# One pool of weight staging buffers for a two-layer hybrid backbone on one core, with feed-forward groups of 512, 512 and 256 tokens

## The chip, the cores and the metric

The kernel runs on 1 core of a Trainium2 chip: TensorE (PE in the rows) multiplies matrices, VectorE (DVE), ScalarE (ACT) and GpSimd (POOL) work elementwise, SyncE (SP) issues the DMA transfers, and 16 DMA engines move data between memory and the core. Each engine works off its own instructions in order and waits on semaphores for the others. The metric is the device time of one execution in microseconds.

## The reference, cut to what matters

```python
for l in range(DEPTH):                       # 2 layers, D_MODEL 1024, D_FF 4096
    mod_l = silu(c) @ w_mod[l] + b_mod[l]    # six vectors: shift, scale, gate, twice; mod_c from c_ctx
    h_l = rms_norm(x, norm1_g[l]) * (1 + sc1_l) + sh1_l        # 1024 latent tokens
    h_c = rms_norm(xc, norm1_g[l]) * (1 + sc1_c) + sh1_c       # 256 context tokens
    pl, pc = split_cols(h_l @ w_in[l]), split_cols(h_c @ w_in[l])
    ...                                      # four mixers: convolution, gated scan, attention, retention
    x = x + g1_l * (concatenate([y_conv, y_gla, y_att, y_ret]) @ w_out[l])
    h2_l = rms_norm(x, norm2_g[l]) * (1 + sc2_l) + sh2_l
    x = x + g2_l * (square(relu(h2_l @ w_up[l])) @ w_down[l])
    if l < DEPTH - 1:
        ...                                  # the same for the context xc
return rms_norm(x, final_norm_g)             # latent tokens only
```

The weights of the second layer's modulation, `w_mod[1]`, are multiplied while the feed-forward of the first layer runs.

## The kernel before

**Tokens and products.** The stream is kept transposed, features on the partitions, in three groups of tokens (`TOK`): t = 0 is the context with 256 tokens, t = 1 and t = 2 hold 512 latent tokens each. Every large fp32 product is done as three matmuls of rounded parts (`mm3`, L189): high times high, high times low, low times high. The trace shows them in the order `ahi,whi`, `alo,whi`, `ahi,wlo` (moving, weights); all matmuls have line L187. In a layer come the projections with the attention, the scans, the output projection and the feed-forward.

**How weights arrive.** `load_slab` (L250) takes a staging tile `wst`, lets SyncE load a slab of weights into it (L258) and calls `split`: ScalarE casts it to the high part `whi` (L180), VectorE subtracts to the low part `wlo` (L181). When the low part is done, the staging tile is free for the next load. In the wide phase (`open_w`: output projection and feed-forward, slabs of 1024 columns, 512 KB) and in the narrow phase (`open_narrow`: projections and attention, slabs of 512 or 544 columns) there are 3 staging tiles, and each phase has its own, in the pool of the weights. The modulation slabs (`stage_w`, L274, named `wm`) go through the same tiles; TensorE reads them straight from the tile in fp32, and the tile is free when those matmuls are done.

**The feed-forward.** The 4096 hidden features are cut into 16 chunks of 256. A unit is one chunk with one token group, in the order chunk, then t = 0, 1, 2 (layer 1 has only t = 1, 2). For each unit the loop takes two steps of the modulation generator `mg` (`emit_mods`, L310; it hands out 8 slabs, one step each, and then one step that evaluates and transposes, six times over, 54 steps in all, which with two steps a unit last through the first nine chunks of layer 0; in layer 1 `mg` is empty). Then it emits `up` of the next unit and `down` of this one:

```python
1199        for i, u_ in enumerate(units):
1200            step(mg, 2)
1201            if i + 1 < len(units):
1202                up(*units[i + 1])
1207            down(*u_)
```

`up` loads the chunk's two w_up slabs when t is the first group, and `down` its two w_down slabs. An up or a down is 48 matmuls of 512 columns (256 for t = 0).

**The layer boundary.** Behind the last chunk, `next_norm` forms the next layer's first norm for each group: ScalarE squares, VectorE adds (L369), TensorE sums over the partitions (`c<-acc,ones`), ScalarE makes the factor (L174), VectorE and ScalarE apply it (L382, L385, L386). Then the attention's slabs come (two granules of four slabs with 512 columns), and `att_in` multiplies them with tiles of 128 tokens: 0 and 1 are the context, 2 to 9 the latents. The order of emission, a little rearranged by a scheduler at build time, is the order on each engine.

Of the kernel before, what the change touches and what calls it, by code (L numbers as in the profile page):

```python
# [8 lines left out]
F32 = mybir.dt.float32  # L9
# [3 lines left out]
ALU = mybir.AluOpType  # L13
# [7 lines left out]
NTILE = NT // 128  # L21
CT = NCTX // 128
FF = 4096
P_IN = 2576
EPS = 1e-6
FC = 256
SLAB = 1024
NSLAB = 544
TOK = [(0, 256), (256, 512), (768, 512)]
C_CONV, C_GLA, C_GLAZ, C_GATE_R, C_ATT, C_RET, C_GATE_G = 0, 512, 1280, 1024, 1296, 1808, 2320  # L30
# [70 lines left out]
def build(tc, a, out, dbg=None):  # L101
    cst = a["cst"]
    nc = tc.nc
    pools = Pools(tc)
    PS = bass.MemoryType.PSUM
    dbg = dbg or {}

    cpool = pools.get("cpool")
    nrm = pools.get("nrm", bufs=2)
    xyp = {}  # L110

    def open_xy():
        xyp[0] = xyp[1] = pools.get("xy01")
        xyp[2] = pools.get("xy2")

    dram = pools.get("dram", space=bass.MemoryType.DRAM)
    P = {}
# [58 lines left out]
            after_(i_, cur["load"])  # L176
            cur["users"].append(i_)

    def split(hi, lo, src):
        nc.scalar.copy(hi, src)  # L180
        nc.vector.tensor_tensor(lo, src, hi.bitcast(F32), op=ALU.subtract)  # L181

    def tr(ps, src, n=128):
        nc.tensor.transpose(ps, src, ident[:n, :n])  # L184
# [52 lines left out]
    W = {}  # L237

    def open_w():
        wp = pools.get("wp", bufs=5)  # L240
        W.update(pools=[wp], group=1, n=0, width=SLAB, st=wp, stages=3)

    def open_narrow(**kw):
        wps = [pools.get(nm, bufs=4, **kw) for nm in ("wpa", "wpb")]
        W.update(pools=wps, group=4, n=0, width=NSLAB, st=wps[0], stages=3)

    def close_narrow():
        pools.close("wpb", "wpa")

    def load_slab(src, k, n):  # L250
        wd_ = W["width"]
        st = W["st"].tile([128, wd_], F32, tag="wst", name="wst", bufs=W["stages"])
        if not isinstance(src, list):
            src = [(src, n)]
        o = 0
        v = st[:, :k * n].rearrange("p (k n) -> p k n", k=k)
        for s, w in src:
            nc.sync.dma_start(out=v[:, :, o:o + w], in_=s)  # L258
            o += w
        p = W["pools"][W["n"] // W["group"] % len(W["pools"])]  # L260
        W["n"] += 1
        hi = p.tile([128, wd_], F32R, tag="whi", name="whi")
        lo = p.tile([128, wd_], F32R, tag="wlo", name="wlo")
        split(hi[:, :k * n], lo[:, :k * n], st[:, :k * n])
        return (hi[:, :k * n].rearrange("p (k n) -> p k n", k=k), lo[:, :k * n].rearrange("p (k n) -> p k n", k=k))

    def granule(l, pieces, width):
        w_in = a["w_in"][l].rearrange("(k p) n -> p k n", p=128)
        return [load_slab([(w_in[:, 2 * q:2 * q + 2, c0:c0 + w], w) for c0, w in pieces], 2, width) for q in range(4)]

    def att_cols(g):
        return [(C_ATT + 128 * g, 128), (C_ATT + 256 + 64 * g, 64), (C_ATT + 384 + 64 * g, 64)]

    def stage_w():  # L274
        v = W["st"].tile([128, W["width"]], F32, tag="wst", name="wm", bufs=W["stages"])
        return v[:, :512 if W["width"] < 1024 else 1024].rearrange("p (k q n) -> p k q n", k=1, q=4)

    vecs = [cpool.tile([128, NV], F32, name=f"vec{l}") for l in range(2)]
    wdw = [cpool.tile([128, 62], F32, name=f"wdw{l}") for l in range(2)]
# [70 lines left out]
    def xy_tile(t, nm):  # L350
        return xyp[t].tile([128, KD, TOK[t][1]], F32, tag=f"xy{t}", name=f"{nm}{t}")
# [43 lines left out]
    xin = pools.get("xin", bufs=2)  # L395
# [49 lines left out]
    for t in (2, 0, 1):  # L445
        for k in range(0, KD, 2):
            nc.sync.dma_start(out=xdram[:, k:k + 2, TOK[t][0]:TOK[t][0] + TOK[t][1]], in_=xt[t][:, k:k + 2, :])
    pools.close("xin", "init", "xy2", "xy01", "psd")

    pace = []  # L450

# [16 lines left out]
    for l in range(2):  # L468
        last = l == 1
# [110 lines left out]
        def att_in(A, i, sls, aa, tb):  # L580
# [55 lines left out]
            nc.sync.dma_start(out=attraw[i][:, h0 * 64:320], in_=ov[:, 1, h0:5, :].rearrange("p h d -> p (h d)"))  # L636
            att_prep(A, i, ov[:, 0].rearrange("p h d -> p (h d)"))

        def att_stage(sls, *others):
            aa = pools.get("aa", bufs=2)  # L640
            tb = {"cos": aa.tile([128, 8, 32], F32, name="cosa", bufs=1), "sin": aa.tile([128, 8, 32], F32, name="sina", bufs=1),
                  "gain": aa.tile([128, 2, 3, 64], F32, name="gain", bufs=1)}
            nc.sync.dma_start(out=tb["cos"].rearrange("p a b -> p (a b)"), in_=cslice("cosatt"))
            nc.sync.dma_start(out=tb["sin"].rearrange("p a b -> p (a b)"), in_=cslice("sinatt"))
            for g in range(2):
                for h_ in range(3):
                    src = a["att_q_norm_g" if h_ < 2 else "att_k_norm_g"][l:l + 1, :]
                    nc.sync.dma_start(out=tb["gain"][:, g, h_, :], in_=src.to_broadcast([128, 64]))
            A = att_tiles()
            for _ in stagger((att_in(A, i, sls, aa, tb) for i in range(NTILE)), 2):  # L650
                for g_ in others:
                    step(g_)
            pools.close("aa")
            return A

        def att_second(A):
            for i in range(NTILE):
                h0 = 0 if need_q(i) else 2
                rw = at_.tile([128, 256], F32, tag="arw", name="arw", bufs=2)
                nc.sync.dma_start(out=rw[:, h0 * 64:256], in_=attraw[i][:, h0 * 64:256])  # L660
                nc.sync.dma_start(out=A["ve"][:, i, :], in_=attraw[i][:, 256:320])
                att_prep(A, i, rw)
                yield
# [7 lines left out]
        def attend(A, g):  # L671
            qa, ka, kb, ve = A["qa"], A["ka"], A["kb"], A["ve"]
            nfill = 0
            for t in order:
# [45 lines left out]
                nc.vector.reciprocal(ls[:, 0:nt, :], ls[:, 0:nt, :])  # L720
                rb = bank("pt")
                for j in range(nt):
                    dg = at_.tile([128, 2, 128], F32, tag="adg", name="adg")
                    nc.vector.tensor_tensor(dg, ident[:, None, :].to_broadcast([128, 2, 128]),
                                            ls[:, j, :].unsqueeze(2).to_broadcast([128, 2, 128]), op=ALU.mult)
                    for h_ in range(2):
                        mm(rb[64 * h_:64 * h_ + 64, j * 128:(j + 1) * 128], ones[:, 0:64], dg[:, h_, :], True, True)
# [6 lines left out]
        n_att = sum(len(tiles_of(t)) * (3 + (CT if t == 0 else NTILE) // 2) + 1 for t in tts)  # L734
        n_tok = sum(TOK[t][1] for t in tts)

        A = att_stage(first if l == 0 else [granule(l, att_cols(g), 256) for g in range(2)], mg)
        at_ = pools.get("at", bufs=2)


# [57 lines left out]
        def gla_in(i, qk):  # L798
# [43 lines left out]
            b = bank("s")  # L842
            for d_ in range(2):
                tr(b[:, d_ * 128:(d_ + 1) * 128], ke[:, d_, :])
            kt = ag.tile([128, 2, 128], F32, tag="ket", name="ket")
            nc.vector.tensor_copy(kt, b[:, 0:256].rearrange("p (a b) -> p a b", a=2))
            yield
            outer(b, 256, kt, st, i, ag, glakv)
# [89 lines left out]
        pools.close("ar", "actp", "at", "ap", "pss", "psa", "psd")  # L938
        close_narrow()
        open_xy()  # L940
        y = [None if last and t == 0 else xy_tile(t, "y") for t in range(3)]
        for t in tts:
            o, n = TOK[t]
            nc.sync.dma_start(out=y[t][:, 4:6, :], in_=yatt[:, :, o:o + n])
# [182 lines left out]
        w_up = a["w_up"][l].rearrange("(k p) n -> p k n", p=128)  # L1127
        w_dn = a["w_down"][l].rearrange("(f p) n -> p f n", p=128)
        NF = FC // 128
        units = [(c, t) for c in range(FF // FC) for t in tts]  # L1130
        wu, wd, hid = {}, {}, {}

        def up(c, t):
            n = TOK[t][1]
            if t == tts[0]:
                wu[c] = [load_slab(w_up[:, :, (c * NF + f) * 128:(c * NF + f + 1) * 128], 8, 128) for f in range(NF)]
            hi, lo = h2[t]
            hh = hp.tile([128, NF, 512], F32R, tag="hh", name="hh")
            hl = hp.tile([128, NF, 512], F32R, tag="hl", name="hl")
            for f in range(NF):  # L1140
                b = bank()
                uh, ul = wu[c][f]
                mm3(b[:, :n], [(uh[:, k, :], ul[:, k, :], hi[:, k, :], lo[:, k, :]) for k in range(KD)])
                rl = ntmp()
                nc.scalar.activation(rl[:, :n], b[:, :n], AF.Relu)  # L1145
                nc.scalar.activation(hh[:, f, :n], rl[:, :n], AF.Square)  # L1146
                nc.vector.tensor_tensor(rl[:, :n], rl[:, :n], rl[:, :n], op=ALU.mult)  # L1147
                nc.vector.tensor_tensor(hl[:, f, :n], rl[:, :n], hh[:, f, :n].bitcast(F32), op=ALU.subtract)
            hid[c, t] = (hh, hl)

        def down(c, t):
            n = TOK[t][1]
            seg = 1 if t == 0 else 0
            if t == tts[0]:
                wd[c] = [load_slab(w_dn[:, c * NF + f:c * NF + f + 1, :], 1, 1024) for f in range(NF)]
            hh, hl = hid.pop((c, t))
            for d in range(8):
                ds = slice(d * 128, (d + 1) * 128)
                b = bank()
                mm3(b[:, :n], [(wd[c][f][0][:, 0, ds], wd[c][f][1][:, 0, ds], hh[:, f, :n], hl[:, f, :n]) for f in range(NF)])  # L1160
                nc.vector.scalar_tensor_tensor(xt[t][:, d, :], b[:, :n], mod(l, 5, d, seg), xt[t][:, d, :], op0=ALU.mult, op1=ALU.add)  # L1161
                if c == FF // FC - 1:
                    if d == 0:
                        acc[t] = nacc()
                    square(acc[t], xt[t][:, d, :], n, d == 0)
# [47 lines left out]
        if "x" in dbg and dbg.get("l", 0) == l:  # L1213
            for t in tts:
                o, n = TOK[t]
                nc.sync.dma_start(out=dbg["x"][:, :, o:o + n], in_=xt[t])
        pools.close("hp", "wp", "xy2", "xy01", "psd")
    pools.close("actp", "dram", "nrm", "cpool")


def _layout(inputs):
# [26 lines left out]
```

## Time and profile before

| | |
|---|---|
| median of 3 runs (lowest, highest) | 3265.65 us (3259.18, 3268.56) |
| the profiled execution, its span | 3255.2 us, 3253.4 us |
| TensorE, VectorE, ScalarE, GpSimd busy | 94%, 51%, 28%, 2% of the span |
| mean granted clock of TensorE | 0.963 of full speed |
| feed-forward of layer 0 | about 883 to 1806.5 us |
| layer boundary | 1806.5 to about 1850 us |
| feed-forward of layer 1 | about 2527 to 3230 us |

Times in the rows are microseconds from the start of the span. A granted clock of 1.00 is 2.4 GHz, 0.50 is 1.2 GHz. A share of busy time is a mean over stages with different limits, so that the stages are to be read one by one. Idle time in brackets behind a row is that of the engine just before the instruction, with what ended it.

### The profile page before, as it was taken

What the parts mean: (1) busy time and instruction counts of PE and PEld (TensorE: products, weight loads), DVE (VectorE), ACT (ScalarE), POOL (GpSimd) and SP (SyncE); (2) the same over time, 40 slices, a digit from 0 to 9 for tenths busy, and PEclk for the clock granted to TensorE, in tenths of its full rate; (3) what the DMA queues carried; (4) which work ended last, traced back from release to release, by engine and by line L of the source; (5) the groups of instructions that cost most, each with busy time, mean ns of one, the idle gap of its engine ahead of it and who ended that gap; (6) DMA issues with size and microseconds to landing.
All of it is one profiled execution on the core that took longest, in us unless ns stands there. A gap on an engine that the chain in (4) does not pass through costs nothing. (4 is left out here: it accounts for less than half of the span.)

```text
span 3253.4 us, 43496 instructions
## 1 busy us (share of the span) xinstructions
PE 3055.0 (94%) x18101; PEld 2446.2 (75%) x18101; DVE 1672.7 (51%) x2660; ACT 912.7 (28%) x1650; POOL 66.0 (2%) x114
## 2 busy tenths in 40 slices
PE   7899899868999999999999799999769999999998
PEld 4777677646888888888888777677537788888887
DVE  4559633343654444444545659633444644444545
ACT  4322343242321121121112433343332221112222
POOL 0200000000000000000000010000000000000000
PEclk8899999878999999999999799999889999999999
DMA  8422412362122222221110310212531211111111
GB/s 267 121 69 90 119 49 71 97 196 94 51 79 85 91 85 78 79 65 39 40 39 1 99 55 30 78 47 72 174 117 58 64 51 41 39 52 52 52 39 52
DMA packets 267230, 250.32 MB, mean 77 GB/s; under 512 B 28258, under 2 KB 227512, under 8 KB 267032
## 3 DMA queue, kind: packets, MB, share of 16 engines
q1 hardware_dynamic: 266616, 246.61, 24.1%
q8 instruction: 142, 2.33, 0.3%
q0 software_dynamic: 416, 0.92, 0.1%
q14 instruction: 56, 0.46, 0.0%
HBM read 200.42 MB, written 47.05 MB: 76 GB/s over the span
## 5 line engine op out<-in xcount | busy, mean ns | idle before, releaser
L187 PE MATMUL bank<-ahi,whi 128*128 128x512 f32 (+1 forms) x2096 | 794.7, 379 | 13.7 <-ACT ahi L180 11.2
L187 PE MATMUL bank<-ahi,wlo 128*128 128x512 f32 (+1 forms) x2096 | 786.3, 376 | 2.5 <-DVE wlo L181 2.5
L187 PE MATMUL bank<-alo,whi 128*128 128x512 f32 (+1 forms) x2096 | 787.3, 376 | 0.0
L1161 DVE SCALAR_TENSOR_TENSOR x<-bank,mods,x 128x512 f32<-128x512 f32 (+1 forms) x640 | 439.2, 695 | 253.1 <-PE bank L187 251.6
L187 PEld LDWEIGHTS bank<-ahi,whi 128*128 128x128 f32 x2096 | 396.6, 189 | 110.2 <-ACT ahi L180 14.0
L187 PE MATMUL bank<-hl,whi 128*128 128x512 f32 (+1 forms) x1280 | 472.1, 369 | 0.0
L187 PE MATMUL bank<-hh,whi 128*128 128x512 f32 (+1 forms) x1280 | 471.6, 368 | 0.0
L187 PE MATMUL bank<-hh,wlo 128*128 128x512 f32 (+1 forms) x1280 | 471.0, 368 | 0.0
L187 PEld LDWEIGHTS bank<-ahi,wlo 128*128 128x128 f32 x2096 | 396.1, 189 | 82.0 <-issue 6.0
L187 PEld LDWEIGHTS bank<-alo,whi 128*128 128x128 f32 x2096 | 396.6, 189 | 75.5 <-issue 5.4
L180 ACT CAST whi<-wst 128x1024 fp32r<-128x1024 f32 (+2 forms) x226 | 199.6, 893 | 675.5 <-PE bank L187 492.5
L181 DVE TENSOR_TENSOR wlo<-wst,whi 128x1024 fp32r<-128x1024 f32 (+2 forms) x226 | 232.3, 1039 | 285.1 <-ACT whi L180 283.1
L1145 ACT ACTIVATE tmp<-bank 128x512 f32<-128x512 f32 (+1 forms) x160 | 88.3, 552 | 659.8 <-PE bank L187 658.4
L187 PEld LDWEIGHTS bank<-hh,whi 128*128 128x128 f32 x1280 | 241.3, 188 | 40.9
L187 PEld LDWEIGHTS bank<-hl,whi 128*128 128x128 f32 x1280 | 241.3, 189 | 40.6 <-issue 0.2
L187 PEld LDWEIGHTS bank<-hh,wlo 128*128 128x128 f32 x1280 | 241.3, 189 | 40.4 <-issue 0.2
L1147 DVE TENSOR_TENSOR tmp<-tmp 128x512 f32<-128x512 f32 (+1 forms) x160 | 102.0, 639 | 312.0 <-ACT hh L1146 310.2
L187 PE MATMUL bank<-whi,ahi 128*128 128x256 f32 (+2 forms) x640 | 197.4, 309 | 8.1 <-ACT whi L180 3.5
L187 PE MATMUL bank<-wlo,ahi 128*128 128x256 f32 (+2 forms) x640 | 191.2, 299 | 0.2 <-DVE wlo L181 0.2
L187 PE MATMUL bank<-whi,alo 128*128 128x256 f32 (+2 forms) x640 | 191.0, 298 | 0.0
L690 DVE TENSOR_REDUCE amx<-S 128x1 f32<-128x1280 f32 (+1 forms) x72 | 98.8, 1372 | 138.3 <-PE S L187 132.7
L520 DVE SCALAR_TENSOR_TENSOR yacc<-u,wdw,yacc 128x1295 f32<-128x1295 f32 (+1 forms) x120 | 168.4, 1421 | 0.8
(214 smaller groups left out, 3094.5 us busy)
## 6 DMA issues: line engine op xcount, KB each, us to landing
wm<-in_w_mod_dram SPq DMA_DIRECT2D x64, 512.0 KB, 3.8
wst<-in_w_up_dram SPq DMA_DIRECT2D x64, 512.0 KB, 3.8
wst<-in_w_down_dram SPq DMA_DIRECT2D x64, 512.0 KB, 4.1
wm<-in_w_mod_dram SPq DMA_DIRECT2D x64, 256.0 KB, 3.0
wst<-in_w_in_dram SPq DMA_DIRECT2D x48, 256.0 KB, 2.9
wst<-in_w_out_dram SPq DMA_DIRECT2D x16, 512.0 KB, 5.3
x<-xdram SPq DMA_DIRECT2D x4, 2048.0 KB
glaf<-gf SPq DMA_DIRECT2D x18, 384.0 KB, 2.5
```

What stands on the lines that cost most here:

```text
L180: nc.scalar.copy(hi, src)
L181: nc.vector.tensor_tensor(lo, src, hi.bitcast(F32), op=ALU.subtract)
L187: nc.tensor.matmul(ps, lhsT=lhsT, rhs=rhs, start=start, stop=stop)
L520: nc.vector.scalar_tensor_tensor(yv, uv, wv, yv, op0=ALU.mult, op1=ALU.add)
L690: nc.vector.reduce_max(mx[:, 0:1], S[:, 0:nk * 128], axis=AX.X)
L1145: nc.scalar.activation(rl[:, :n], b[:, :n], AF.Relu)
L1147: nc.vector.tensor_tensor(rl[:, :n], rl[:, :n], rl[:, :n], op=ALU.mult)
L1161: nc.vector.scalar_tensor_tensor(xt[t][:, d, :], b[:, :n], mod(l, 5, d, seg), xt[t][:, d, :], op0=ALU.mult, op1=ALU.add)
```

## The change

1. **One staging pool** `wst` for the whole program, with 2 tiles of 1088 columns. `stage_cols` hands out parts of a tile: slabs of 512 or 544 columns share one, two to a tile; a slab of 1024 columns (all of the feed-forward, its modulation slabs too) takes a whole one. So there are 2 stages instead of 3 in the wide phase and 4 half ones instead of 3 in the narrow phase.
2. **One pool** `xy` for the stream's tiles instead of two.
3. **The groups of layer 0's feed-forward** come as t = 1, 2, 0 (512, 512, 256 tokens) instead of 0, 1, 2. In layer 1 the attention's token tiles come as 2 to 9, then 0 and 1.
4. **The low parts** of layer 1's eight attention slabs are formed by GpSimd instead of VectorE.
5. **A pad** of 480 bytes a partition, and one buffer instead of two for three helpers (`arw` in the second half of the attention, `adg`, `ket`).

```diff
+STAGE = 1088
+    pools.get("pad", side="right").tile([128, 120], F32, name="pad")
     nrm = pools.get("nrm", bufs=2)
+    wstp = pools.get("wst", bufs=2)
     def open_xy():
-        xyp[0] = xyp[1] = pools.get("xy01")
-        xyp[2] = pools.get("xy2")
+        xyp[0] = xyp[1] = xyp[2] = pools.get("xy")
...
-    def split(hi, lo, src):
+    def split(hi, lo, src, lo_eng=None):
         nc.scalar.copy(hi, src)
-        nc.vector.tensor_tensor(lo, src, hi.bitcast(F32), op=ALU.subtract)
+        (lo_eng or nc.vector).tensor_tensor(lo, src, hi.bitcast(F32), op=ALU.subtract)
...
-        W.update(pools=[wp], group=1, n=0, width=SLAB, st=wp, stages=3)
+        W.update(pools=[wp], group=1, n=0, width=SLAB)
...
+    def stage_cols(n):
+        free = W.get("free")
+        if free is None or free[1] + n > STAGE:
+            free = [wstp.tile([128, STAGE], F32, tag="wst", name="wst"), 0]
+        v = free[0][:, free[1]:free[1] + n]
+        free[1] += n
+        W["free"] = free if free[1] < STAGE else None
+        return v
...
     def stage_w():
-        v = W["st"].tile([128, W["width"]], F32, tag="wst", name="wm", bufs=W["stages"])
-        return v[:, :512 if W["width"] < 1024 else 1024].rearrange("p (k q n) -> p k q n", k=1, q=4)
+        n = 512 if W["width"] < 1024 else 1024
+        return stage_cols(n).rearrange("p (k q n) -> p k q n", k=1, q=4)
...
+        tile_order = list(range(NTILE)) if l == 0 else list(range(CT, NTILE)) + list(range(CT))
...
-        A = att_stage(first if l == 0 else [granule(l, att_cols(g), 256) for g in range(2)], mg)
+        A = att_stage(first if l == 0 else [granule(l, att_cols(g), 256, nc.gpsimd) for g in range(2)], mg)
...
+        mt = [1, 2] if last else [1, 2, 0]
...
-        units = [(c, t) for c in range(FF // FC) for t in tts]
+        units = [(c, t) for c in range(FF // FC) for t in mt]
...
-            if t == tts[0]:
+            if t == mt[0]:
```

SyncE's issues at the first chunk boundary of layer 0's feed-forward, before. The number behind a name is the tile's own; `wm` are modulation slabs, three tiles turn over:

```order
L258 DMA wst_7901<-in_w_down_dram 128x1024
L323 DMA wm_7971<-in_w_mod_dram 128x4x256
L323 DMA wm_7977<-in_w_mod_dram 128x4x256
L323 DMA wm_8109<-in_w_mod_dram 128x4x256
L323 DMA wm_8115<-in_w_mod_dram 128x4x256
L258 DMA wst_8121<-in_w_up_dram 128x8x128
L258 DMA wst_8127<-in_w_up_dram 128x8x128
```

The same place after; now two tiles turn over, and all slabs bear the name `wst`:

```order
L269 DMA wst_7849<-in_w_down_dram 128x1024
L334 DMA wst_7919<-in_w_mod_dram 128x4x256
L334 DMA wst_7925<-in_w_mod_dram 128x4x256
L334 DMA wst_8057<-in_w_mod_dram 128x4x256
L334 DMA wst_8063<-in_w_mod_dram 128x4x256
L269 DMA wst_8069<-in_w_up_dram 128x8x128
L269 DMA wst_8075<-in_w_up_dram 128x8x128
```

The sequence is the same; what is other is the number of tiles, so that `wst_8069` and `wst_8075` stand two issues behind `wst_8057` and `wst_8063`, whose tiles they take.

TensorE at that boundary, before: the end of the down of group 1, the two modulation slabs, and the first matmuls with the new w_up slab, on the context's 256 tokens:

```order
L187 MATMUL bank_8101<-hl_7834,whi_7903 128x512
L187 MATMUL bank_8101<-hh_7833,wlo_7904 128x512
L187 MATMUL mo_7820<-wm_8109,scT_84 32x256 x4
L187 MATMUL mo_7820<-wm_8115,scT_84 32x256 x4
L187 MATMUL bank_8135<-ahi0_7400,whi_8123 128x256
L187 MATMUL bank_8135<-alo0_7401,whi_8123 128x256
L187 MATMUL bank_8135<-ahi0_7400,wlo_8124 128x256
```

And after, where the first group is t = 1 with 512 tokens:

```order
L189 MATMUL bank_8049<-hl_7782,whi_7851 128x512
L189 MATMUL bank_8049<-hh_7781,wlo_7852 128x512
L189 MATMUL mo_7768<-wst_8057,scT_91 32x256 x4
L189 MATMUL mo_7768<-wst_8063,scT_91 32x256 x4
L189 MATMUL bank_8083<-ahi1_7502,whi_8071 128x512
L189 MATMUL bank_8083<-alo1_7503,whi_8071 128x512
L189 MATMUL bank_8083<-ahi1_7502,wlo_8072 128x512
```

Directly behind the matmuls that read `wst_8057` and `wst_8063` stand those that need the slabs loaded into the same tiles.

TensorE at the layer boundary, before: the last down, the sum for the norm of group 2, and the first attention matmuls, on the context:

```order
L187 MATMUL bank<-hl,whi 128x512
L187 MATMUL bank<-hh,wlo 128x512
L187 MATMUL c_14666<-acc,ones 128x512
L187 MATMUL bank<-whi,ahi_14351 128x128 x2
L187 MATMUL bank<-wlo,ahi_14351 128x128
```

And after, where the first attention tile holds latent tokens:

```order
L189 MATMUL bank<-hl,whi 128x256
L189 MATMUL c_14489<-acc,ones 128x512
L189 MATMUL bank<-hh,wlo 128x256
L189 MATMUL c_14615<-acc,ones 128x256
L189 MATMUL bank<-whi,ahi_14299 128x256 x2
```

ScalarE there, after (`ahi_14487` is the normed group 2, `ahi_14613` group 0):

```order
L396 ACTIVATE ahi_14487<-tmp,mods_96 128x512 x8
L379 ACTIVATE tmp<-x_6821 128x256 x7
L176 ACTIVATE acc<-c_14615,eps 128x256
L176 ACTIVATE acc<-acc 128x256
L396 ACTIVATE ahi_14613<-tmp,mods_96 128x256 x8
L182 CAST whi<-wst 128x512 x8
```

Two sums now stand ahead of the attention on TensorE, the last that of the small group, and the eight casts stand behind both norms; before, the first cast stood between the two activations of the last norm.

## Rows read from the trace of the kernel before

**Rows 1.** The page: span, and TensorE's busy time, share and instructions.
```profile
span 3253.4 us, 43496 instructions
PE 3055.0 (94%) x18101; PEld 2446.2 (75%) x18101; DVE 1672.7 (51%) x2660; ACT 912.7 (28%) x1650; POOL 66.0 (2%) x114
```

**Rows 2.** Chain of waits, its last long link: start, length, engine, tile, line, instructions.
```profile
2528.25 692.27 PE bank L187 x3005
```

**Rows 3.** Stretches: busy time (instructions) by engine, granted clock, DMA share, GB/s.
```profile
core 0: us, PE busy (x) PEld busy (x) DVE busy (x) ACT busy (x) POOL busy (x), PEclk, DMA share, GB/s
883.00:1806.50 923.50, 923.45 (x5012) 770.65 (x5010) 458.77 (x717) 189.60 (x297) 0.00 (x0) 1.00 0.20 64
...
1811.50:1824.00 12.50, 2.08 (x2) 0.50 (x2) 8.75 (x13) 6.72 (x11) 0.00 (x0) 0.51 0.75 242
1824.00:1848.50 24.50, 21.62 (x95) 20.71 (x96) 17.19 (x31) 11.30 (x23) 0.69 (x2) 0.50 0.37 87
1848.50:1852.50 4.00, 4.00 (x20) 4.00 (x20) 1.41 (x7) 1.21 (x6) 0.56 (x2) 0.50 0.08 25
1852.50:1900.10 47.60, 46.37 (x385) 45.28 (x384) 25.09 (x80) 15.76 (x55) 16.09 (x20) 1.00 0.11 35
```

**Rows 4.** TensorE at a chunk boundary: start, length, line, operation, out<-in.
```profile
908.18 1.07 PE L187 MATMUL mo<-wm,scT 128*32 128x256 f32 x16
909.18 0.50 PE L187 MATMUL bank<-ahi,whi 128*128 128x512 f32 x1
909.51 0.40 PE L187 MATMUL bank<-alo,whi 128*128 128x512 f32 x1
909.75 0.40 PE L187 MATMUL bank<-ahi,wlo 128*128 128x512 f32 x1
...
932.48 0.39 PE L187 MATMUL bank<-ahi,whi 128*128 128x256 f32 x1
932.70 0.28 PE L187 MATMUL bank<-alo,whi 128*128 128x256 f32 x1
932.82 0.28 PE L187 MATMUL bank<-ahi,wlo 128*128 128x256 f32 x1
```

**Rows 5.** SyncE's queue, three issues of w_up slabs (the last of two).
```profile
909.34 0.46 SPq L258 DMA_DIRECT2D wst<-in_w_up_dram  x1
...
968.99 0.37 SPq L258 DMA_DIRECT2D wst<-in_w_up_dram  x1
...
1027.04 0.99 SPq L258 DMA_DIRECT2D wst<-in_w_up_dram  x2
```

**Rows 6.** ScalarE, the casts that follow those issues.
```profile
913.88 1.05 ACT L180 CAST whi<-wst 128x1024 fp32r<-128x1024 f32 x1 [9.60 <-DMA wst<-in_w_up_dram]
...
972.82 1.05 ACT L180 CAST whi<-wst 128x1024 fp32r<-128x1024 f32 x1 [9.82 <-DMA wst<-in_w_up_dram]
...
1031.05 1.05 ACT L180 CAST whi<-wst 128x1024 fp32r<-128x1024 f32 x1 [9.08 <-DMA wst<-in_w_up_dram]
```

**Rows 7.** VectorE, the low part of the first of them.
```profile
914.97 1.22 DVE L181 TENSOR_TENSOR wlo<-wst,whi 128x1024 fp32r<-128x1024 f32 x1 [6.16 <-ACT whi L180]
```

**Rows 8.** Two short gaps of TensorE, and stretches behind them (columns as in rows 3).
```profile
1921.78 0.90 PE L184 MATMUL pt<-ident,aP 128*128 128x128 f32 x3 [3.17 <-ACT aP L174]
...
2428.93 0.80 PE L187 MATMUL bank<-ahi,whi 128*128 128x512 f32 x1 [5.70 <-ACT ahi L180]
...
2428.90:2432.90 4.00, 3.97 (x9) 2.86 (x10) 3.99 (x7) 4.00 (x8) 0.00 (x0) 0.50 0.42 137
...
1921.60:1928.00 6.40, 6.22 (x25) 4.95 (x26) 2.75 (x4) 2.50 (x5) 0.00 (x0) 0.51 0.01 4
```

**Rows 9.** The layer boundary on TensorE, VectorE and ScalarE.
```profile
1820.96 2.08 PE L187 MATMUL c<-acc,ones 128*128 128x512 f32 x2 [14.12 <-DVE acc L369]
1824.32 0.69 PE L187 MATMUL bank<-whi,ahi 128*128 128x128 f32 x2 [1.28 <-ACT whi L180]
...
1802.08 1.40 DVE L382 SCALAR_TENSOR_TENSOR tmp<-x,msc,acc 128x512 f32<-128x512 f32 x2
...
1823.66 0.61 ACT L180 CAST whi<-wst 128x512 fp32r<-128x512 f32 x1
```

**Rows 10.** Groups by form: busy time, mean ns of one, idle before.
```profile
L181 DVE TENSOR_TENSOR wlo<-wst,whi 128x512 fp32r<-128x512 f32 x74 | 51.5, 703 | 35.9 <-ACT whi L180 34.0 <-PE pt L184 1.5
...
L369 DVE TENSOR_TENSOR acc<-acc,tmp 128x256 f32<-128x256 f32 x14 | 5.9, 421 | 1.8 <-ACT tmp L368 1.6
...
L528 POOL TENSOR_TENSOR tmp<-yacc 128x512 f32<-128x512 f32 x4 | 5.3, 1330 | 158.9 <-DVE yacc L520 155.5 <-PE s L187 3.4
```

**Rows 11.** Scan starts: SyncE's queue in layer 1; TensorE's waits there, both layers.
```profile
2324.68 0.55 SPq L258 DMA_DIRECT2D wst<-in_conv_w_pw_dram  x1
...
PE c L187 <- ACT shi L180: 12.0, 2, 10.6
...
PE c L187 <- ACT shi L180: 8.6, 2, 7.5
```

More of the change, by code (lines that the diff above doesn't have):

```diff
@@ L240, in open_w, with load_slab @@
         wp = pools.get("wp", bufs=5)
-        W.update(pools=[wp], group=1, n=0, width=SLAB, st=wp, stages=3)
+        W.update(pools=[wp], group=1, n=0, width=SLAB)
     def open_narrow(**kw):
         wps = [pools.get(nm, bufs=4, **kw) for nm in ("wpa", "wpb")]
-        W.update(pools=wps, group=4, n=0, width=NSLAB, st=wps[0], stages=3)
+        W.update(pools=wps, group=4, n=0, width=NSLAB)
     def close_narrow():
         pools.close("wpb", "wpa")
-    def load_slab(src, k, n):
+    def stage_cols(n):
[6 more added lines that the diff above has]
+        return v
+    def load_slab(src, k, n, lo_eng=None):
         wd_ = W["width"]
-        st = W["st"].tile([128, wd_], F32, tag="wst", name="wst", bufs=W["stages"])
+        st = stage_cols(k * n)
         if not isinstance(src, list):
@@ L255, in load_slab @@
         o = 0
-        v = st[:, :k * n].rearrange("p (k n) -> p k n", k=k)
+        v = st.rearrange("p (k n) -> p k n", k=k)
         for s, w in src:
@@ L263, in load_slab, with granule @@
         lo = p.tile([128, wd_], F32R, tag="wlo", name="wlo")
-        split(hi[:, :k * n], lo[:, :k * n], st[:, :k * n])
+        split(hi[:, :k * n], lo[:, :k * n], st, lo_eng)
         return (hi[:, :k * n].rearrange("p (k n) -> p k n", k=k), lo[:, :k * n].rearrange("p (k n) -> p k n", k=k))
-    def granule(l, pieces, width):
+    def granule(l, pieces, width, lo_eng=None):
         w_in = a["w_in"][l].rearrange("(k p) n -> p k n", p=128)
-        return [load_slab([(w_in[:, 2 * q:2 * q + 2, c0:c0 + w], w) for c0, w in pieces], 2, width) for q in range(4)]
+        return [load_slab([(w_in[:, 2 * q:2 * q + 2, c0:c0 + w], w) for c0, w in pieces], 2, width, lo_eng) for q in range(4)]
     def att_cols(g):
@@ L447, in build @@
             nc.sync.dma_start(out=xdram[:, k:k + 2, TOK[t][0]:TOK[t][0] + TOK[t][1]], in_=xt[t][:, k:k + 2, :])
-    pools.close("xin", "init", "xy2", "xy01", "psd")
+    pools.close("xin", "init", "xy", "psd")
     pace = []
@@ L649, in att_stage @@
             A = att_tiles()
-            for _ in stagger((att_in(A, i, sls, aa, tb) for i in range(NTILE)), 2):
+            for _ in stagger((att_in(A, i, sls, aa, tb) for i in tile_order), 2):
                 for g_ in others:
@@ L658, in att_second @@
                 h0 = 0 if need_q(i) else 2
-                rw = at_.tile([128, 256], F32, tag="arw", name="arw", bufs=2)
+                rw = at_.tile([128, 256], F32, tag="arw", name="arw", bufs=1)
                 nc.sync.dma_start(out=rw[:, h0 * 64:256], in_=attraw[i][:, h0 * 64:256])
@@ L722, in attend @@
                 for j in range(nt):
-                    dg = at_.tile([128, 2, 128], F32, tag="adg", name="adg")
+                    dg = at_.tile([128, 2, 128], F32, tag="adg", name="adg", bufs=1)
                     nc.vector.tensor_tensor(dg, ident[:, None, :].to_broadcast([128, 2, 128]),
@@ L844, in gla_in @@
                 tr(b[:, d_ * 128:(d_ + 1) * 128], ke[:, d_, :])
-            kt = ag.tile([128, 2, 128], F32, tag="ket", name="ket")
+            kt = ag.tile([128, 2, 128], F32, tag="ket", name="ket", bufs=1)
             nc.vector.tensor_copy(kt, b[:, 0:256].rearrange("p (a b) -> p a b", a=2))
@@ L940, in build @@
         open_xy()
-        y = [None if last and t == 0 else xy_tile(t, "y") for t in range(3)]
+        mt = [1, 2] if last else [1, 2, 0]
+        y = {t: xy_tile(t, "y") for t in mt}
         for t in tts:
@@ L1153, in down @@
             seg = 1 if t == 0 else 0
-            if t == tts[0]:
+            if t == mt[0]:
                 wd[c] = [load_slab(w_dn[:, c * NF + f:c * NF + f + 1, :], 1, 1024) for f in range(NF)]
@@ L1216, in build @@
                 nc.sync.dma_start(out=dbg["x"][:, :, o:o + n], in_=xt[t])
-        pools.close("hp", "wp", "xy2", "xy01", "psd")
-    pools.close("actp", "dram", "nrm", "cpool")
+        pools.close("hp", "wp", "xy", "psd")
+    pools.close("actp", "dram", "wst", "nrm", "cpool", "pad")
 def _layout(inputs):
```

## The prediction

> **What bounds the kernel now.** I read the page's head first: TensorE is busy for 3055.0 of 3253.4 us, so whatever makes it wait lengthens the run, and whatever another engine does beside it costs nothing [rows 1]. The chain of waits says the same from the other end: its last long link is one unbroken stretch of 692.27 us of TensorE in the second feed-forward [rows 2]. Then I cut the trace by stage. In the feed-forward of layer 0, 883 to 1806.5 us, TensorE is busy for 923.45 of 923.50 us at a granted clock of 1.00 [rows 3]: there is nothing to gain there, and every wait that is put there is paid in full. Behind it lies the layer boundary, where TensorE is nearly empty and then runs at half clock until 1852.5 us [rows 3]; that is the one larger piece in the parts that the change touches which could be won back. Last I read one chunk boundary of that feed-forward operation by operation, because the staging tiles turn over there.
>
> **How a weight slab gets to TensorE.** A chunk needs two w_up slabs. SyncE issues a slab's load when its staging tile is free, ScalarE casts it, VectorE forms the low part, and only then can the third matmul of `mm3` run. The reader should see three loads in the rows: issues at 909.34, 968.99 and 1027.04 us [rows 5], casts at 913.88, 972.82 and 1031.05 us [rows 6]. From issue to cast that is 4.54, 3.83 and 4.01 us. The third is the one with both slabs issued at once, as they are after the change. The cast takes 1.05 us [rows 6] and the low part 1.22 us [rows 7]. None of it costs anything now: the load of 909.34 us was issued right behind the modulation matmuls of 908.18 us, and the matmuls that use the slab begin at 932.48 us, one full unit (an up and a down) later [rows 4].
>
> **The change: two staging tiles instead of three (the large term).** In the first nine chunks of layer 0 two modulation slabs go through the same tiles between any two units. Counting SyncE's issues back: with three tiles the first w_up slab takes a tile whose modulation slab was consumed a unit earlier (in the build, the second w_up slab then follows in the same tile). With two tiles the two w_up slabs take exactly the tiles of the two modulation slabs issued just before them, and those are consumed by the small modulation matmuls that stand in TensorE's order immediately ahead of the matmuls that need the new slabs. So the load cannot start before TensorE is there, and TensorE, in order, has nothing else to do. One stall, from rows:
> - issue to cast 4.01 us (ends 3.83 and 4.54) [rows 5, 6];
> - the cast, 1.05 us [rows 6];
> - the low part, 1.22 us, less the two matmuls that need only the high part, 0.24 us each (909.51 to 909.75 us) [rows 4, 7]: 0.75 us;
> - less the second modulation slab, which TensorE still works off meanwhile: half of 1.07 us, 0.53 us [rows 4].
>
> That is 4.01 + 1.05 + 0.75 - 0.53 = 5.3 us idle. The second slab is cast about 2 us behind the first and needed after 24 matmuls of 0.23 us, 5.6 us: hidden. The gaps of similar length show what follows an idle TensorE. After the gap of 5.70 us before 2428.93 us the clock is 0.50 for 4.0 us of almost solid work [rows 8], so 2.0 us are lost; after a wait of 3.17 us it is 0.51 for 6.4 us, 6.22 of them busy [rows 8], so 3.1 us. I take 2.0, since the 5.70 us gap is the nearest in length, with 0 and 3.1 as ends. One stall is then 7.3 us, between 3.83 + 1.05 - 0.53 = 4.35 and 4.54 + 1.05 + 0.75 - 0.53 + 3.1 = 8.9.
>
> How many: the boundaries at which a full pair of modulation slabs stands ahead of w_up. In the order after the change these are six (chunks 0, 1, 3, 4, 6, 7 to the next). At the other three of the nine, one of the pair is the evaluation step with its two transposes; the tile is free a unit early there, as before. From chunk 9 on, and in all of layer 1, no modulation slabs are loaded: the w_up slabs then take the tiles of w_down, released a unit earlier, and two tiles do. The w_down slabs wait for the first modulation pair, but have the next up (48 matmuls of 0.23 us, 11.2 us) to land in against about 6.3 us needed. **6 x 7.3 = 43.8 us**, ends 26 and 53.5.
>
> In sentences that the sum can do without: the Trainium skill, "DMA: Bandwidth & Descriptors" (Anatomy of one DMA), gives about 2.0 us fixed plus bytes over 436 GB/s, an estimate of 3.2 us for 512 KB where the rows show 3.83 to 4.54 to the cast; by it a stall would be 6.5 us and six of them 39. The same page's rules for kernel authors say to issue a load early and wait for it late, which is what the six loads lose here; the trace of before agrees, with 23 us between issue and use.
>
> **The layer boundary.** Before, TensorE waits 14.12 us for the sums of squares of group 2 [rows 9], then works off the two context tiles of 48 matmuls in 24.5 us at half clock [rows 3]; the eight latent tiles run from 1848.5 to 1900.1 us. After: group 2's last updates come one 256-token down (about 5.9 us) earlier, but group 0's sums stand on VectorE behind the whole application of group 2's norm: 16 operations of 0.70 us [rows 9], 11.3 us. Then 7 additions of 0.42 [rows 10], the column sum with two activations on ScalarE (3 us, as from 1820.96 to 1823.66 us [rows 9]), and 16 operations at 0.42 for group 0 (an estimate from the row of the additions). On ScalarE the eight casts of the attention slabs now stand behind all of that, on TensorE group 0's column sum stands ahead of the first attention matmul. 3 (group 2's own sum and activations) + 11.3 + 2.9 + 3 + 6.7 = 27 us, plus a cast of 0.6 [rows 9] and a low part of 1.33 us on GpSimd [rows 10]: TensorE resumes some 30 us after 1806.6, at 1836.5, against 1824 before [rows 9]. GpSimd needs 1.33 us a slab where VectorE needs 0.70 [rows 10], but four slabs (5.3 us) serve 48 matmuls of 0.12 us (932.70 to 932.82 us [rows 4]) at full and about twice that at half clock, so that it stays ahead after the first. From 1836.5 the eight latent tiles take the same 51.6 us, and the two context tiles, now last and at full clock, at most 5.8 each (a context tile has half the columns; the 48 matmuls of 256 columns take that): 1836.5 + 51.6 + 11.6 = 1899.7 against 1900.1. **Taken as 0**; ends -8 (context tiles at half that, casts overlapping the norm) and +10 (half clock over the first two tiles).
>
> **The rest.** Early staging: the first slab of a phase no longer waits for the pools of the last to close; ahead of the scans that moves a load with its 0.55 us of SyncE's queue out of the way of the z loads behind it [rows 11], about 0.5 us a layer: **-1**. The output projection of layer 0 loads its fourth second-half slab one low part later: **+0.7**. The order 512, 512, 256 makes the second unit wait for group 2's norm, as layer 1 does already with hardly a gap: **+1**. Half tiles in the narrow phases give four slots instead of three, released in pairs: 0, since every slab keeps at least its old distance. The single buffers of the attention and scan helpers, and the pad: 0, ends -3 and +3; their operations lie on VectorE (51% busy before) beside matmuls.
>
> Sum: 43.8 + 0 - 1 + 0.7 + 1 = 44.5 us. On the profiled execution (3255.2 us) that gives 3299.7. That execution lies 10.45 us under the median of the runs shown, 3265.65, so that I forecast 3265.65 + 44.5 = **3310**.
>
> **Rivals.**
> - *Stalls, but no clock loss* (chance 0.17): 6 x 5.3 = 32, so 3298. For it: the work around these gaps is denser than around the two gaps in rows 8. Against it: of those two one was shorter than a stall here and one about as long, and the clock fell after both.
> - *Two tiles are enough* (0.10): the loads are hidden, because the order on the chip is looser than I count, and nothing but the small terms is left, 3266. The Trainium skill, "Trainium Kernel Development and Optimization" (Best Practices), says to double-buffer so that loads overlap compute; no run here shows two tiles yet. Against it: the two w_up slabs come directly behind the two modulation slabs on the same tiles, and a wait on a matmul in TensorE's own order cannot be looser.
> - *Earlier loads win at the phase starts* (faster, 0.05): with a staging pool that stays open, the slabs of the attention and of the scans are on chip before their phase begins. The place is the layer boundary and the scan starts; the price is at most the 42 us from 1806.6 to 1848.5 less the 11.6 that the context tiles need, 30, and the waits of TensorE on the convolution's split at the scan starts, 8.6 and 12.0 us [rows 11], at most some 18 together. -48 beats the stalls only if they are below 38, that is, without the clock loss; at their low end of 26 it gives 3244. Against it: the boundary's first wait ends with VectorE's sums, not with a load [rows 9], and that queue gets longer.
> - *The boundary gets worse* (0.08): the casts behind the norm cost 20 us instead of 0, with the stalls: 3331.
>
> **How the numbers follow.** The forecast has 0.60, the rivals 0.17, 0.10, 0.05 and 0.08. Range: from the low ends together (26 - 8 - 3 = 15) over the fastest of the runs shown (3259.18), 3274, a little further for the second rival's side, to the high ends together (53.5 + 10 + 3 + 1.7 = 68) over the median, 3334: 3270 to 3334. A measurement of this kernel can tell about 0.3% (10 us) from no change. Faster by more than that is the third rival and a remnant, 0.06; within it the second, 0.09; slower 0.85.
>
> **What would show it.** In the changed kernel's trace: six gaps of TensorE of 4.4 to 6 us between 883 and 1850 us, each right behind modulation matmuls and ended by a cast of a w_up slab, with a granted clock of 0.5 for some 4 to 6 us behind it; a w_up issue within half a microsecond of the modulation matmuls at those six places, and none such in layer 1. At the boundary TensorE should resume some 30 us after the last feed-forward matmul, with latent tiles, ended by a low part on GpSimd. I am wrong if the first feed-forward shows no such gaps, if they number nine or three, if the clock stays at 1.00 through them, or if the boundary moves by more than 10 us.

## The result, and the profile after

The change makes the kernel a little slower: 3281.56 us in the median of 6 runs (3276.98 to 3287.25) against 3266.46 for the kernel before (3259.18 to 3269.21), a ratio of 1.0052 with a 95% interval of 1.0036 to 1.0067. The forecast was +44.5 us and 3310 us; measured are +15.1 us. The profiled executions differ by more, 3253.4 against 3280.4 us of span, since that of before was one of its quickest.

By stages, the trace of after shows the forecast's largest term nearly at the forecast's size, and a gain that the forecast had put at nothing. This is the page's head of the kernel after, to be read beside [rows 1]: span and instructions, then busy time by engine.

```profile
span 3280.4 us, 43486 instructions
PE 3038.8 (93%) x18101; PEld 2447.0 (75%) x18101; DVE 1670.2 (51%) x2652; ACT 914.6 (28%) x1650; POOL 76.8 (2%) x122
```

TensorE is busy for 16.2 us *less* than before with the same 18101 instructions, although the clock is lower for longer. The work itself got shorter, and idle time grew by more.

The first feed-forward of after, TensorE's waits from 880 to 1860 us (engine, tile, line, for whom; us in total, times, longest):

```profile
PE bank L189 <- ACT whi L182: 28.5, 6, 5.0
PE bank L189 <- DVE x L1175: 2.7, 3, 1.6
```

Six waits for a cast, 4.75 us each in the mean (4.53 to 4.97). One of them, on TensorE, SyncE, ScalarE and VectorE (start, length, engine, line, operation; in brackets the idle time ahead and what ended it):

```profile
935.35 1.07 PE L189 MATMUL mo<-wst,scT 128*32 128x256 f32 x16
941.10 0.79 PE L189 MATMUL bank<-ahi,whi 128*128 128x512 f32 x1 [4.68 <-ACT whi L182]
...
936.05 0.99 SPq L269 DMA_DIRECT2D wst<-in_w_up_dram  x2
...
940.00 1.04 ACT L182 CAST whi<-wst 128x1024 fp32r<-128x1024 f32 x1 [14.62 <-DMA wst<-in_w_up_dram]
...
941.08 1.22 DVE L183 TENSOR_TENSOR wlo<-wst,whi 128x1024 fp32r<-128x1024 f32 x1 [4.87 <-ACT whi L182]
```

The first w_up load is issued while the modulation matmuls ahead of it still run, the second right behind them. The first cast starts 3.95 us after the first issue, and TensorE, which had the slab a whole unit early in [rows 4 to 6], stands still until that cast is done. The same place in stretches (columns as in [rows 3]):

```profile
936.20:939.40 3.20, 0.22 (x5) 0.00 (x0) 0.01 (x1) 0.00 (x0) 0.00 (x0) 1.00 0.61 167
939.40:946.30 6.90, 5.16 (x11) 3.64 (x12) 2.45 (x2) 2.09 (x2) 0.00 (x0) 0.51 0.60 174
946.30:952.00 5.70, 5.70 (x26) 4.69 (x25) 1.17 (x2) 1.23 (x2) 0.00 (x0) 1.00 0.18 63
```

The granted clock falls to its lower level 3 us into the gap and stays there until 946.3 us, over 5.16 us of busy time, of which half, 2.6 us, is lost. Over the six gaps 1.9 to 3.2 us are lost in this way, 2.6 in the mean, so that idle time and half clock make 28.5 + 15.6 = 44.1 us.

Where the other sign comes from is seen in the second feed-forward, where nothing of the order changed. The first pair of lines is a stretch of 200 us in each kernel, before and then after (busy time and number of matmuls first); the second pair, from 2650 to 3200 us, shows two groups of before and the same two of after, by form (number, busy time, mean ns of one):

```profile
2600.00:2800.00 200.00, 200.00 (x870) 163.12 (x869) 95.32 (x125) 38.13 (x53) 0.00 (x0) 1.00 0.14 43
```

```profile
2640.00:2840.00 200.00, 200.00 (x884) 165.65 (x883) 96.75 (x126) 39.75 (x54) 0.00 (x0) 1.00 0.15 47
```

```profile
L187 PE MATMUL bank<-ahi,whi 128*128 128x512 f32 x397 | 157.1, 396 | 0.0
L187 PE MATMUL bank<-hh,whi 128*128 128x512 f32 x400 | 155.8, 390 | 0.0
```

```profile
L189 PE MATMUL bank<-hh,whi 128*128 128x512 f32 x409 | 159.1, 389 | 0.0
L189 PE MATMUL bank<-ahi,whi 128*128 128x512 f32 x400 | 155.6, 389 | 0.0
```

TensorE is busy throughout at full clock in both, yet gets through 884 matmuls instead of 870. The matmuls that stream the normed activations (`ahi`, `alo`) were 6 to 7 ns longer than those that stream the hidden ones (`hh`, `hl`); after the change both are alike. From start to start that is 233.4 ns before and 226.7 after for `ahi` and `alo`, and 227 and 226.7 for `hh` and `hl`. In the chain of waits the stretch of [rows 2], 692.27 us for 3005 instructions, is now

```profile
2576.92 670.57 PE bank L189 x2957
```

that is 230.4 ns an instruction before and 226.8 after.

### The profile page after: what moved, and what is told of

Same layout as the page of the kernel before. It is cut to its first block, busy times and chain, and to the rows that moved or that the text cites. A ratio compares the mean times of both kernels' runs of the same rounds, so it can differ in the third digit from the quotient of the medians.

```text
span 3280.4 us, 43486 instructions
## 1 busy us (share of the span) xinstructions
PE 3038.8 (93%) x18101; PEld 2447.0 (75%) x18101; DVE 1670.2 (51%) x2652; ACT 914.6 (28%) x1650; POOL 76.8 (2%) x122
## 4 chain that ended last, share of the span: by engine, by line
PE 73%; DMA 3%; DVE 3%; ACT 2%; issue 2%; SPq 0%; POOL 0%; DVEq 0%; ACTq 0%; POOLq 0%
PE bank L189 63%; PE ob L189 2%; PE S L189 2%; PE pt L186 1%; PE sc L189 1%; PE s L189 1%; PE oo L189 1%; DMA wst<-in_w_up_dram 1%; PE mo L189 1%; DMA wst<-in_w_out_dram 1%; PE c L189 1%; ACT whi L182 0%; DMA rx<-retf 0%; ACT fsq L176 0%; DVE alo L397 0%
## 5 line engine op out<-in xcount | busy, mean ns | idle before, releaser
L1175 DVE SCALAR_TENSOR_TENSOR x<-bank,mods,x 128x512 f32<-128x512 f32 (+1 forms) x640 | 439.6, 695 | 243.8 <-PE bank L189 243.1
L1161 DVE TENSOR_TENSOR tmp<-tmp 128x512 f32<-128x512 f32 x160 | 101.9, 638 | 390.6 <-ACT hh L1160 388.8
L1159 ACT ACTIVATE tmp<-bank 128x512 f32<-128x512 f32 x160 | 88.4, 553 | 737.3 <-PE bank L189 735.7
```

## The experiments

The new theory is that the pad does it: before, `ahi` and `alo` start 480 bytes past a multiple of 512, after the 480 bytes of pad at a multiple of 512; `hh` and `hl` start at a multiple in both (these are the addresses that the build gives the tiles). The rival is that the merged pools do it. The old theory on the stalls and its rivals were put to the test in the same runs. The runs were made on several chips. Where two of them are compared, the difference is given as it stands and, in brackets, with each taken against the kernel before on its own chip.

**e1: the pad taken out of the kernel after.**

```diff
-    pools.get("pad", side="right").tile([128, 120], F32, name="pad")
```

> The changed kernel without the 480-byte pad, nothing else altered; the normed activations (ahi, alo), which TensorE streams as the moving operand of w_up and w_out, start at 480 past a multiple of 512 bytes again, as before the change. Theory (the start address of the moving operand sets the pitch of a matmul): 512-column matmuls with ahi and alo go from 226.7 back to 233 ns, some 3840 of them, so about +24 us: 3281.6 + 24 = 3306 us; the matmuls of w_down (hh, hl) stay at 226.7. Rival (the faster matmuls come from the one staging pool or the merged stream pool, that is from other places of weights and loads): 226.7 ns stay, no change, 3282 us.

Measured: 3307.62 us (ratio to before 1.0135, 1.0099 to 1.0171). In the second feed-forward (2650 to 3200 us, by form):

```profile
L188 PE MATMUL bank<-ahi,whi 128*128 128x512 f32 x400 | 158.2, 396 | 0.0
L188 PE MATMUL bank<-hh,whi 128*128 128x512 f32 x397 | 154.7, 390 | 0.0
```

The long matmuls are back, and the six gaps are the same (28.5 us). Without the pad the change costs 44 us (3307.6 against 3263.8 for before on this chip), close to the forecast's sum of 44.5.

**e2: the pad alone in the kernel before** (one buffer for `ket` makes the room; three staging tiles, the old order).

```diff
+    pools.get("pad", side="right").tile([128, 120], F32, name="pad")
-            kt = ag.tile([128, 2, 128], F32, tag="ket", name="ket")
+            kt = ag.tile([128, 2, 128], F32, tag="ket", name="ket", bufs=1)
```

> The kernel before with the 480-byte pad alone (and one buffer instead of two for ket, which makes the room for it); three staging tiles, the old group order. Theory (address): matmuls with ahi and alo fall from 233 to 227 ns, about -24 us: 3266.5 - 24 = 3242 us, with no gap in the first feed-forward. Rival (staging pool): 233 ns stay, 3266 us.

Measured: 3238.33 us against 3263.82, ratio 0.9925 (0.9898 to 0.9951), 25.5 us less. The two groups in the second feed-forward (2650 to 3200 us):

```profile
L188 PE MATMUL bank<-hh,whi 128*128 128x512 f32 x407 | 158.5, 389 | 0.0
L188 PE MATMUL bank<-ahi,whi 128*128 128x512 f32 x400 | 155.6, 389 | 0.0
```

From the start of the last gap ahead of the layer-1 output projection to the start of the gap ahead of the final norm's sums are 803.0 us (2410.47 to 3213.46) against 815.2 before (2423.23 to 3238.38), and there is no gap over 1.5 us in the first feed-forward. The rival is out: no pool was merged here, and the tiles of the weights lie where they lay before. The single buffer of `ket` has no part in it either, for e8 gains as much without it (25.4 us in its one run).

**e3: the modulation steps behind the next up.**

```diff
         for i, u_ in enumerate(units):
-            step(mg, 2)
             if i + 1 < len(units):
                 up(*units[i + 1])
+            step(mg, 2)
```

> The changed kernel with one edit: in the feed-forward loop the two modulation steps are emitted behind the next unit's up instead of ahead of it, so that the tiles that w_up takes were consumed one down (11.1 us) earlier. Theory (six stalls, each 4.75 us idle and about 2.6 us lost at half clock, and a low part): the six gaps go, 3281.6 - 6 x 7.5 = about 3236 us. Rival (the gaps cost only their idle time): 3281.6 - 28.5 = 3253 us. Rival (the loop's length is set elsewhere, the gaps only move): 3282 us.

Measured: 3293.95 us, slower than the kernel after by about 12 (15 against before on its own chip), and none of the three expectations in time; the third had the gaps move, but at no cost. TensorE's waits from 880 to 1860 us, then one place in that stretch on TensorE and SyncE:

```profile
PE bank L189 <- ACT whi L182: 36.7, 11, 4.5
```

```profile
908.37 1.07 PE L189 MATMUL mo<-wst,scT 128*32 128x256 f32 x16
913.81 0.50 PE L189 MATMUL bank<-hh,whi 128*128 128x512 f32 x1 [4.37 <-ACT whi L182]
...
909.07 1.72 SPq L269 DMA_DIRECT2D wst<-in_w_down_dram  x2
```

The six gaps at w_up are gone; nine new ones of 3.1 to 4.5 us stand at w_down, in each of the nine chunks with modulation work. The modulation matmuls now stand right ahead of `down`, whose two slabs take the tiles that they free. The mechanism held; my edit moved it to the other pair of loads.

**e4: two staging tiles in the wide phase of the kernel before**, nothing else.

```diff
-        W.update(pools=[wp], group=1, n=0, width=SLAB, st=wp, stages=3)
+        W.update(pools=[wp], group=1, n=0, width=SLAB, st=wp, stages=2)
```

> The kernel before with two staging tiles instead of three in the wide phase and nothing else. Theory (two tiles make the six stalls by themselves): six gaps of 4.5 to 5 us behind modulation matmuls, half clock behind each, 3266.5 + 45 = 3311 us. Rival (the new group order is needed for the stalls): no gaps, 3266 us.

Measured: 3307.88 us against 3263.82, +44.1, ratio 1.0132 (1.0095 to 1.017). TensorE's waits from 880 to 1860 us:

```profile
PE bank L187 <- ACT whi L180: 28.1, 6, 4.8
PE bank L187 <- DVE wlo L181: 2.9, 6, 0.6
```

The number of tiles alone makes the six gaps; group order, merged pools and GpSimd are not needed for them. 44.1 / 6 = 7.35 us a stall, if all of the difference is put down to them.

**e5: the steps placed by what the next up loads.**

```diff
+            loads = i + 1 < len(units) and units[i + 1][1] == mt[0]
+            if not loads:
+                step(mg, 2)
             if i + 1 < len(units):
                 up(*units[i + 1])
+            if loads:
+                step(mg, 2)
```

> The changed kernel with the modulation steps behind the next unit's up only where that up loads new w_up slabs, ahead of it elsewhere. Theory (a stall is a load whose tile is freed right ahead of its use): w_up then takes tiles freed a unit (11 to 17 us) earlier, w_down keeps an up of 11 us between its tiles' release and its use; neither the six gaps at w_up nor the nine at w_down: 3281.6 less six times 7.5 to 8, about 3235 us. Rival (two tiles are too few for four loads a unit at any order): gaps appear elsewhere, and the time stays above 3270 us.

Measured: 3240.0 us, ratio to before 0.9925 (0.9905 to 0.9944), 41.6 us less than the kernel after (41.3 against before on its own chip). From 880 us to the layer boundary no wait for a cast is left. Two tiles do here, if no load's tile is freed right ahead of the load's use.

**e6, e7, e8: smaller pads in the kernel before** (8, 24 and 56 columns of 4 bytes, as the first line of e2, with `ket` as before; one run each).

> The kernel before with a pad of 32 bytes: the normed activations start at 448 past a multiple of 512, that is at a multiple of 64. Theory 512 (only a multiple of 512 gives the short pitch): 512-column matmuls with ahi, alo at 233 ns in the second feed-forward, no change of time. Theory 64 (a multiple of 64 is enough): 226.7 ns, some 24 us less.

> The kernel before with a pad of 96 bytes: the normed activations start at 384 past a multiple of 512, a multiple of 128. Theory 512: 233 ns. Theory 64 or 128: 226.7 ns, some 24 us less.

> The kernel before with a pad of 224 bytes: the normed activations start at 256 past a multiple of 512. Theory 512: 233 ns. Theory 64, 128 or 256: 226.7 ns, some 24 us less.

Measured: 3259.2, 3267.1 and 3240.74 us. The same group by form in each, in this order:

```profile
L188 PE MATMUL bank<-ahi,whi 128*128 128x512 f32 x400 | 157.7, 394 | 0.0
```

```profile
L188 PE MATMUL bank<-ahi,whi 128*128 128x512 f32 x400 | 157.9, 395 | 0.0
```

```profile
L188 PE MATMUL bank<-ahi,whi 128*128 128x512 f32 x401 | 156.1, 389 | 0.0
```

Starts at 448 and 384 past a multiple of 512 are long, 256 past is short. Of the steps named, neither 512 nor 64 or 128 bytes fits; 256 is the one that separates these cases. The single time of e6 lies at the fast end of the runs of before (3259.51 to 3270.06 us on that chip), and its matmuls are the long ones.

**e9: the hidden activations moved instead** (the kernel of e5 with 128 bytes ahead of `hh` and `hl`).

```diff
         hp = pools.get("hp", bufs=2)
+        hp.tile([128, 32], F32, name="shift", bufs=1)
```

> The kernel of e5 with the hidden activations of the feed-forward (hh, hl, the moving operand of w_down) moved by 128 bytes, by a 128-byte tile ahead of them in their pool; the normed activations stay at a multiple of 512 and the weights where they were. Theory (the moving operand's own start address sets the pitch): now the 512-column matmuls with hh and hl take 233 ns and those with ahi and alo keep 226.7; 3072 of them by 6.5 ns is +20 us: 3240 + 20 = 3260 us. Rival (the pad works through something else that lies on the right side of the memory): all stay at 226.7, 3240 us.

Measured: 3256.89 us, ratio to before 0.9978 (0.9964 to 0.9992), 17 us above e5 (20 with each against before on its own chip, as forecast). The same two groups:

```profile
L189 PE MATMUL bank<-hh,whi 128*128 128x512 f32 x398 | 157.1, 395 | 0.0
...
L189 PE MATMUL bank<-ahi,whi 128*128 128x512 f32 x400 | 155.7, 389 | 0.0
```

Now `hh` is long and `ahi` short, with the weights where they were. It is the moving operand's own start address, on either side of the memory.

**e10: the attention's low parts on VectorE again.**

```diff
-        A = att_stage(first if l == 0 else [granule(l, att_cols(g), 256, nc.gpsimd) for g in range(2)], mg)
+        A = att_stage(first if l == 0 else [granule(l, att_cols(g), 256) for g in range(2)], mg)
```

> The changed kernel with the low parts of layer 1's first attention slabs on VectorE again instead of GpSimd. Theory of the sum (GpSimd is hidden there): the layer boundary moves by under 3 us, 3281.6 within 3. Rival (GpSimd's slower operation sets the boundary's end): faster by about 4 us, 3277. Rival (GpSimd relieves VectorE, which is the bound there): slower by 5 us, 3287.

Measured: 3278.38 us, ratio to before 1.0048 (1.0033 to 1.0063), beside 1.0052 (1.0036 to 1.0067) for the kernel after: no difference clear of the noise. The two gaps at the boundary are the same to 0.01 us (16.47 and 8.54).

## Why the prediction was right in sign and wrong in size

**The stalls: right.** Six gaps, at the chunks named, each behind modulation matmuls and ended by a w_up cast, none in layer 1. Worked out were 7.3 us each and 43.8 together. The chip gave 44.1 with two tiles as the only edit (e4) and 41.6 when the kernel after was freed of them (e5). The parts of the gap shown above: 3.95 us from issue to cast against 4.01 forecast, 1.04 for the cast, 4.75 us idle in the mean, and 2.6 us of half clock in the mean against 2.0 taken. What came out smaller was the wait for the low part: it is done at 942.30 us, 1.2 us after the first matmul, but at half clock the first two matmuls fill most of that, so that about 0.3 us and not 0.75 are left. The load itself took longer than the 3.2 us that the Trainium skill's "DMA: Bandwidth & Descriptors" (Anatomy of one DMA) leads one to estimate for 512 KB; the measured 3.95 us to the cast decides. The Trainium skill gives that figure for transfers that GpSimd issues, and SyncE issues these, so that it was no estimate for them in the first place.

**The layer boundary: right.** Forecast were a first attention matmul 30 us after the last one of the feed-forward and no change by the end of the attention tiles. TensorE's two gaps after the change, on the 256-token group's column sum and on the first cast, from 1847 to 1941 us:

```profile
PE c L189 <- DVE acc L380: 16.5, 1, 16.5
PE bank L189 <- ACT whi L182: 8.6, 1, 8.6
PE bank L189 <- ACT aov L608: 2.6, 6, 0.6
PE bank L189 <- POOL wlo L183: 0.6, 1, 0.6
```

From the end of the feed-forward at 1847.97 us the attention begins at 1874.21, 26 us later, with latent tiles, and its last tile ends at about 1941.2: 93.2 us, against 93.5 before (1806.6 to 1900.1, [rows 3]). The wait of 14.12 us in [rows 9] became 16.5 + 8.6 us, and full clock over the context tiles pays for it. What ended the wait was a cast, not GpSimd's low part as forecast: GpSimd holds TensorE up for 0.6 us, and e10 shows that it decides nothing. Two smaller waits are in no term of the sum. One is the 2.7 us for VectorE (L1175), in the rows of waits above; it falls into the last downs of layer 0's feed-forward. The other stands behind the last attention tile, where the first projection waits 4.2 us for ScalarE, and 0.4 us before the change:

```profile
1945.73 0.80 PE L189 MATMUL bank<-ahi,whi 128*128 128x512 f32 x1 [4.21 <-ACT aov L608]
```

That projection begins 97.8 us after the feed-forward's end, against 94.2 before, still inside the 10 us that the forecast allowed the boundary.

**The pad: wrong, and nearly the whole error.** The step that failed is the sentence that put "the single buffers [...] and the pad" at 0 with ends of -3 and +3. It was the term with the second largest size: -25.5 us (e2); the kernel after and e1 differ by 26 us (28.7 with each against before on its own chip). Put in place of the 0, -25.5 makes the sum 44.5 - 25.5 = 19 us, against the 15.1 measured. That 3281.56 us lies inside the stated range is luck: its low end stood for stalls without a loss of clock and a boundary 8 us shorter, and neither came. I took an edit that moves no instruction for one that moves no time, and looked only at which instructions run when, not at how long one takes and why. The trace of before had it in view: in one and the same stretch matmuls of one shape took 396 ns with one operand and 390 with another (the rows above). Two groups of one form with different means ask for a reason, and the operands' addresses are one of the few things in which they differ.

**The rivals.** "Stalls, but no clock loss" falls with the stretch of 0.51 behind each gap. "Two tiles are enough" is false for this order and true for another (e5). "Earlier loads win" has no place in the trace: the longest wait for the convolution's split in layer 1 is 9.4 us instead of 10.6, 1 us. "The boundary gets worse" falls with the 93.2 us above (its 3331 should be 3330: 3310 + 20).

**Versions that beat both.** The kernel before with the pad (e2, 3238 us) and the kernel after with the steps placed by load (e5, 3240 us) are both some 0.75% faster than before; one keeps three tiles, the other two.

## What to carry to other kernels

Compare matmuls of one shape by their operands, in a stretch at full clock: where one operand's are a few per cent longer, look at its start address before at anything else, and let it start at a multiple of 256 bytes, the step that separated the cases here. When buffers are taken away, write down for each load whose use frees its buffer; here a load whose buffer was freed by the instruction right ahead of its own use cost its whole latency and a spell of half clock, and changing the order of emission was enough to part the two. After such an edit count the other loads too (e3).

## What the runs showed of the hardware that I had not expected

In the second feed-forward, at full clock, a 512-column matmul whose moving operand starts at 480, 448, 384 or 128 bytes past a multiple of 512 takes 233 ns from start to start; at 0 or 256 past it takes 226.7, nearly 3% less. Five of these cases are `ahi` and `alo` (e2, before, e6, e7, e8), 128 is `hh` and `hl` (e9). Whether it is the start or each 2 KB row that must lie so can't be told here, since the rows of these tiles follow each other at multiples of 512 bytes. Why it is so, no row shows. The projections' 512-column matmuls keep some 231 ns in the kernel after, although their `ahi` starts at a multiple of 512; that was not followed up. One difference is seen in the kernel: the weight tiles there are 544 columns (2176 bytes) wide, so that neighbours start 128 bytes apart past a multiple of 512, where those of the feed-forward all start at a multiple. Whether the weights' start has a part in it was not tested.
